# Query norms in a one-core transformer block: the squares move through TensorE instead of being its weights

## The chip, the cores and the metric

The kernel runs on one core of one Trainium2 chip. The metric is the device time of one execution in microseconds (us); the time before is the median of three runs, 1139.22 us (1139.1 to 1141.05). A profile is taken of one execution. Its engines are TensorE (PE; its weight loads are listed as PEld), VectorE (DVE), ScalarE (ACT), GpSimd (POOL) and SyncE (SP), which here only issues DMAs. A matrix product on TensorE has a stationary operand, which is loaded first, and a moving one, which streams through it column by column; results go to one of eight banks of PSUM, from which VectorE and ScalarE read. [...]

## The reference

A block of 512 tokens and 1024 features: a gated feed-forward layer, a mixer, another feed-forward layer. In the mixer two attentions ("moba" and "dsa", eight heads of 64 each) work on projections of the normed input. The change concerns how the queries of both are normed:

```python
qa = rmsnorm(qa.reshape(B, S, N_HEADS_DSA, HEAD_DIM), q_norm_dsa[l])
qb = rmsnorm(qb.reshape(B, S, N_HEADS_MOBA, HEAD_DIM), q_norm_moba[l])
# rmsnorm(x, g) = x * rsqrt(mean(x * x, over the 64 of a head) + EPS) * g
```

Everything is float32. In "dsa" each query attends to its best keys by a second score (128 of them), in "moba" to blocks of keys; both add a bias by distance and take a softmax.

## The kernel before, in words

Activations lie with features on partitions and the 512 tokens along the free dimension. A product in float32 precision is made of three products in the faster fp32r type: operands are split into a rounded high part and the remaining low part (`mm3`, lines 125 to 128: high x high, high x low, low x high). Weights come by DMA into `raw` (three buffers, `wunit`, line 121), ScalarE rounds them into `whi` (line 111), and GpSimd subtracts to get `wlo` (line 117), in the attentions in pieces of 256 columns. A projection `unit` (line 389) is eight such triplets into one PSUM bank, and `post` then reads the bank out.

PSUM's eight banks form rings: `mm` has three (projections and the key norms' sums), `s` two (the logits of the attention), `pt` two (transposes, the query norms' sums, small things), `o` one. A scratch ring of SBUF, `tmp`, has seven buffers of 128x512 (TMPS, line 30); a tile is given back when its last reader is done. Who wants a tile while none is free waits.

TensorE's instructions stand in the order in which the program is written (line 85). `weave` (line 712) interleaves the attention's logits, transposes and values with the steps of a list of projections, the filler. One step is one triplet of a projection (two in the value units), and each step ticks a clock (`tick`, line 379). `later(n, fn)` runs `fn`, and so puts its TensorE instructions there, n steps after now. The instructions of the other engines and SP are put in an order by a planner with modelled times and priorities ahead of the run, and each engine then executes its own strictly in that order: an instruction that waits holds all behind it.

Each head pair of each attention has one key unit and one query unit, eight query units in all. `k_post` (line 462) squares the keys, splits the squares into two parts, and after LAG = 11 steps two products of 512 columns with the block matrix `bd` (1/64 on each head's diagonal block, lines 475 and 476) give the means, spread over all partitions. `q_post` (line 426) is different: the norm isn't applied to q. q goes unnormed into the logits, and the factor of each query enters in the softmax step (`f`, a scale in line 628) and its inverse in the bias addend (`inv`, lines 602 to 605). Both are needed with queries on partitions. So LAG_Q = 4 steps after `q_post`, `norm` (line 438) uses each 128x128 block of the squares as the stationary operand and two columns of `bd` as the moving one, in plain float32; sums of queries on partitions, for both heads of the pair, then stand in a `pt` bank, 128x8. Six small VectorE instructions (lines 444 to 451) and two ScalarE ones turn them into `f` and `inv`.

The softmax sums at line 628 feed the exponential, the transposes (line 659, `turn`) and the values (lines 680 and 681). Row sums of the softmax take a way through DRAM already: `norms` (line 633) writes a row (line 642) and reads it back spread over partitions (line 646).

Of the kernel before, what the change touches and what calls it, by code (L numbers as in the profile page):

```python
# [11 lines left out]
F32 = mybir.dt.float32  # L12
F32R = mybir.dt.float32r
AF = mybir.ActivationFunctionType
ALU = mybir.AluOpType

P = 128
S = 512
D = 1024
F = 2816  # L20
DH = 64
# [4 lines left out]
NQ = S // P  # L26
# [5 lines left out]

PIN, EVERY = (0, 20, 28, 31), 2

LAG, LAG_Q = 11, 4

SPIN, HURRY = 10, 200

# [7 lines left out]
def f32(ap):  # L46
    return ap.bitcast(F32)
# [3 lines left out]
def block_kernel(ctx, tc, x, gains, wgu1, wd1, w_in, w_v, wb_a, wb_b, w_out, wgu2, wd2, rel_bias, onehot, out):  # L51
    nc = tc.nc

    def pool(name, bufs=1, **kw):
        return ctx.enter_context(tc.tile_pool(name=name, bufs=bufs, **kw))
# [4 lines left out]
    dr = pool("dr", space=bass.MemoryType.DRAM)  # L60
# [21 lines left out]
    def log_exp(out, src, fn, **k):  # L82
        table_op("natural_log_exp_and_others", out, src, fn, **k)
# [3 lines left out]
    def T(tag, bufs, shape=(P, S), dt=F32, p=sb):  # L87
        uid[0] += 1
        return p.tile(list(shape), dt, tag=tag, name=f"{tag}{uid[0]}", bufs=bufs)

    def tmp(dt=F32):
        return T("tmp", TMPS, (P, S), dt)

    def mmps():
        return T("mm", 3, p=ps)
# [4 lines left out]
    def tps():  # L100
        return T("pt", 2, p=ps)
# [60 lines left out]
    bd = cp.tile([P, P], F32R, name="bd")  # L162
# [27 lines left out]
    def blocks(a):  # L190
        return a.rearrange("p (t c) -> p t c", c=P)

    def rev(a):

        o = a[:, P - 1:P]
        return bass.AP(o.tensor, o.offset, [list(o.ap[0]), [P, NQ], [-1, P]])
# [49 lines left out]
    whole, halves = (slice(0, S),), (slice(0, S // 2), slice(S // 2, S))  # L246
# [129 lines left out]
    def later(n, fn):  # L376
        late.append((steps[0] + n, fn))
# [48 lines left out]
    def q_post(p, gain, dst):  # L426


        sq = tmp()
        nc.scalar.activation(blocks(sq), rev(p), AF.Square)  # L430
        q = T("q", 2, (P, 2, S), F32R)
        for e, h1 in enumerate(HALF):
            h2, g = HALF[1 - e], gain[h1]
            nc.scalar.activation(blocks(q[h1, e, :]), rev(p)[h1], AF.Copy, scale=g)
            nc.vector.scalar_tensor_tensor(blocks(q[h2, e, :]), rev(p)[h1], g, blocks(f32(q)[h1, e, :]),
                                           op0=ALU.mult, op1=ALU.subtract)

        def norm():
            pv = tps()[:, 0:2 * NQ]
            for t in range(NQ):  # L440
                nc.tensor.matmul(pv[:, 2 * t:2 * t + 2], sq[:, t * P:(t + 1) * P], f32(bd)[:, 0:P:DH],
                                 start=True, stop=True)
            w, y, b, f, inv = (a for a in T("fq", 3, (P, 5, 2 * NQ)).rearrange("p n c -> n p c"))
            nc.vector.tensor_mul(w, pv, r2q[:, 1])
            log_exp(y, w, AF.Ln, bias=epst)
            log_exp(y, y, AF.Exp, scale=-0.5)
            nc.vector.scalar_tensor_tensor(b, w, EPS, y, op0=ALU.add, op1=ALU.mult)
            nc.vector.tensor_mul(b, b, y)
            nc.vector.scalar_tensor_tensor(b, b, -3.0, y, op0=ALU.add, op1=ALU.mult)
            nc.vector.scalar_tensor_tensor(f, b, -0.5, r2q[:, 0], op0=ALU.mult, op1=ALU.mult)  # L450
            nc.vector.reciprocal(inv, f)
            dst.extend([q, f, inv])

        later(LAG_Q, norm)

    lows = [cp.tile([P, 2, S], F32R, name=f"low{i}") for i in range(2)]
    for low in lows:
        for e in range(2):
            nc.gpsimd.memset(f32(low)[HALF[1 - e], e, :], 0.0)
    turns = [0, 0]  # L460

    def k_post(p, gain, dst):

# [61 lines left out]
    def qk_units(br, pr, q, k):  # L525
        u = (U_QA, U_QB)[br] + pr
        g = 2 * br
        return [proj(u + 4, lambda p: k_post(p, gqk[:, g + 1:g + 2], k)),
                proj(u, lambda p: q_post(p, gqk[:, g:g + 1], q))]
# [237 lines left out]
    p = tps()  # L767
# [9 lines left out]
    for e in range(2):  # L777
        nc.vector.tensor_copy(r2q[:, 0, e:2 * NQ:2], p[:, NQ:2 * NQ])
    nc.vector.tensor_mul(r2q[:, 1], r2q[:, 0], r2q[:, 0])
    q_post(ps3[0], gqk[:, 2:3], moba[0][0])  # L780
    k_post(ps3[1], gqk[:, 3:4], moba[0][1])
    run(v0)
# [35 lines left out]
    for c in range(KD):  # L818
        g1 = opened(c)
        ma = tmp()  # L820
        w = ready.pop(0)
# [88 lines left out]
```

## Time and profile before

| | |
|---|---|
| median of three runs | 1139.22 us (1139.1 to 1141.05) |
| profiled execution | 1139.47 us, span 1137.7 us |
| PE busy | 1130.0 us, 5364 products |
| PEld busy | 947.0 us |
| DVE, ACT, POOL busy | 646.2, 469.9, 549.3 us |
| DMA | 111.73 MB, mean 98 GB/s |
| eight query norms | between 385 and 664 us |

The span is the time from the first to the last instruction of the profiled execution. Matrix products are pipelined, and the ends that the profile shows are modelled; what a product costs TensorE is read from the distance of its start to the start of the next one. A row of the time-ordered view has the start, the length, the engine, the line, the tiles it writes and reads, the shape and a count; a bracket at its end has the engine's idle time before it and the instruction that ended it.

### The profile page before, as it was taken

What the parts mean: (1) busy time and instruction counts of PE and PEld (TensorE: products, weight loads), DVE (VectorE), ACT (ScalarE), POOL (GpSimd) and SP (SyncE); (2) the same over time, 40 slices, a digit from 0 to 9 for tenths busy, and PEclk for the clock granted to TensorE, in tenths of its full rate; (3) what the DMA queues carried; (4) which work ended last, traced back from release to release, by engine and by line L of the source; (5) the groups of instructions that cost most, each with busy time, mean ns of one, the idle gap of its engine ahead of it and who ended that gap; (6) DMA issues with size and microseconds to landing.
All of it is one profiled execution on the core that took longest, in us unless ns stands there. A gap on an engine that the chain in (4) does not pass through costs nothing.

```text
span 1137.7 us, 14242 instructions
## 1 busy us (share of the span) xinstructions
PE 1130.0 (99%) x5364; PEld 947.0 (83%) x5364; DVE 646.2 (57%) x971; ACT 469.9 (41%) x770; POOL 549.3 (48%) x435
## 2 busy tenths in 40 slices
PE   9999999999999999999999999999999999999998
PEld 8888888888888888888889888888888888888887
DVE  6853156613557458699958785754663156613641
ACT  6432123312325568768238766444332123212321
POOL 3444444444446574665564551174444444444443
PEclk9999999999999999999999999999999999999999
DMA  7233222322323222321232321422233232322322
GB/s 237 94 118 95 93 97 105 95 93 93 106 71 114 83 101 84 102 75 52 98 131 93 110 67 47 139 93 97 103 98 93 93 105 100 93 93 96 104 70 102
DMA packets 39580, 111.73 MB, mean 98 GB/s; under 512 B 4534, under 2 KB 9048, under 8 KB 39512
## 3 DMA queue, kind: packets, MB, share of 16 engines
q1 hardware_dynamic: 39080, 110.28, 29.4%
q8 instruction: 42, 0.69, 0.2%
q10 hardware_dynamic: 432, 0.55, 0.2%
q14 instruction: 26, 0.21, 0.1%
HBM read 108.64 MB, written 2.17 MB: 97 GB/s over the span
## 4 chain that ended last, share of the span: by engine, by line
PE 92%; DVE 5%; ACT 2%; issue 1%; POOL 1%; POOLq 0%; DVEq 0%
PE mm L126 22%; PE mm L127 22%; PE mm L128 22%; PE s L126 7%; PE s L128 7%; PE s L127 7%; PE pt L659 1%; DVE l L628 1%; PE s L619 1%; PE s L620 1%; DVE work L566 1%; PE o L681 1%; PE o L680 1%; POOL wlo L117 1%; DVE pt L670 0%
## 5 line engine op out<-in xcount | busy, mean ns | idle before, releaser
L117 POOL TENSOR_TENSOR wlo<-raw,whi 128x256 fp32r<-128x256 f32 (+2 forms) x344 | 491.6, 1449 | 528.7 <-ACT whi L111 517.4
L111 ACT ACTIVATE whi<-raw 128x1024 fp32r<-128x1024 f32 (+2 forms) x206 | 203.8, 994 | 509.5 <-PE mm L127 325.8
L126 PE MATMUL mm<-x,whi 128*128 128x512 f32 x630 | 249.6, 396 | 1.1 <-DVE v L501 1.1
L128 PE MATMUL mm<-x,wlo 128*128 128x512 f32 x630 | 245.9, 390 | 0.0
L127 PE MATMUL mm<-x,whi 128*128 128x512 f32 x630 | 245.9, 390 | 0.0
L126 PE MATMUL mm<-a,whi 128*128 128x512 f32 (+1 forms) x462 | 178.5, 386 | 0.0
L127 PE MATMUL mm<-a,whi 128*128 128x512 f32 (+1 forms) x462 | 178.5, 386 | 0.0
L128 PE MATMUL mm<-a,wlo 128*128 128x512 f32 (+1 forms) x462 | 178.4, 386 | 0.0
L128 PEld LDWEIGHTS mm<-x,wlo 128*128 128x128 f32 x630 | 118.2, 188 | 25.3
L126 PEld LDWEIGHTS mm<-x,whi 128*128 128x128 f32 x630 | 118.4, 188 | 22.8 <-DVE v L501 1.6
L127 PEld LDWEIGHTS mm<-x,whi 128*128 128x128 f32 x630 | 118.5, 188 | 21.3 <-DVE x L207 0.4
L126 PE MATMUL s<-x,whi 128*128 128x512 f32 x342 | 133.1, 389 | 0.0
L128 PE MATMUL s<-x,wlo 128*128 128x512 f32 x342 | 133.0, 389 | 0.0
L127 PE MATMUL s<-x,whi 128*128 128x512 f32 x342 | 133.0, 389 | 0.0
L289 DVE SCALAR_TENSOR_TENSOR h<-mm,h 128x512 f32<-128x512 f32 (+1 forms) x49 | 33.3, 681 | 167.6 <-PE mm L128 167.6
L275 DVE TENSOR_TENSOR tmp<-tmp,tmp 128x512 f32<-128x512 f32 x44 | 97.0, 2205 | 30.4 <-ACT tmp L75 30.1
L154 DVE TENSOR_TENSOR a<-tmp,a 128x512 fp32r<-128x512 f32 x49 | 86.4, 1764 | 28.5 <-ACT a L153 28.3
L126 PEld LDWEIGHTS mm<-a,whi 128*128 128x128 f32 x462 | 86.8, 188 | 17.6
L127 PEld LDWEIGHTS mm<-a,whi 128*128 128x128 f32 x462 | 86.8, 188 | 17.6
L128 PEld LDWEIGHTS mm<-a,wlo 128*128 128x128 f32 x462 | 86.8, 188 | 17.6
L128 PEld LDWEIGHTS s<-x,wlo 128*128 128x128 f32 x342 | 64.2, 188 | 13.4
L126 PEld LDWEIGHTS s<-x,whi 128*128 128x128 f32 x342 | 64.2, 188 | 13.3
(196 smaller groups left out, 1361.8 us busy)
## 6 DMA issues: line engine op xcount, KB each, us to landing
raw<-in_ffn_w_gu_dram SPq DMA_DIRECT2D x84, 512.0 KB, 3.5
raw<-in_w_in_dram SPq DMA_DIRECT2D x35, 512.0 KB, 3.5
raw<-in_ffn_w_down_dram SPq DMA_DIRECT2D x32, 512.0 KB, 3.5
raw<-in_ffn_w_down_dram SPq DMA_DIRECT2D x16, 384.0 KB, 3.1
bias<-fd SPq DMA_DIRECT2D x16, 256.0 KB, 3.4
raw<-in_w_v_dram SPq DMA_DIRECT2D x8, 512.0 KB, 3.4
raw<-in_w_out_dram SPq DMA_DIRECT2D x8, 512.0 KB, 3.5
raw<-in_ffn_w_gu_dram SPq DMA_DIRECT2D x16, 128.0 KB, 3.9
```

The costliest lines, as they stand in the source:

```text
L111: nc.scalar.activation(hi, raw, AF.Copy)
L117: eng.tensor_sub(lo[:, b], raw[:, b], f32(hi)[:, b])
L126: nc.tensor.matmul(pt, wh, xh, start=start, stop=False)
L127: nc.tensor.matmul(pt, wh, xl, start=False, stop=False)
L128: nc.tensor.matmul(pt, wl, xh, start=False, stop=stop)
L154: nc.vector.tensor_sub(lo, src, f32(hi))
L275: nc.vector.tensor_mul(g1, g1, s)
L289: nc.vector.scalar_tensor_tensor(h[c][:, b], pd, 0.5, h[c][:, b], op0=ALU.mult, op1=ALU.add)
L566: nc.vector.match_replace(out=acc, in_to_replace=m8, in_values=acc, imm_value=-2e38)
L619: nc.tensor.matmul(p[:, 0:N], qb, k[:, e, 0:N], start=True, stop=False)
L620: nc.tensor.matmul(p[:, 0:N], qb, kl[:, e, 0:N], start=False, stop=True)
L628: sums[i] = nc.vector.tensor_tensor_reduce(out=pe, in0=p[:, 0:W], in1=pe, scale=f[:, 2 * qt + e:2 * qt + e + 1], scalar=3e38, op0=ALU.add, ...
```

## The change

The squares are now split in a high and a low part, as for the keys: ScalarE copies them to fp32r, GpSimd subtracts in two halves. After seven steps instead of four, the two parts move, 512 columns each, against the two columns of `bd`; the result is 2x512, a head per partition, in a bank of the `mm` ring. ScalarE copies it to SBUF, SP writes it to one of two DRAM rows, and four steps later `factors` reads it back by two DMAs, one element a piece, to 128x8 in SBUF. The rest of the arithmetic is unchanged.

```diff
-LAG, LAG_Q = 11, 4
+LAG, LAG_Q, LAG_R = 11, 7, 4
...
         sq = tmp()
         nc.scalar.activation(blocks(sq), rev(p), AF.Square)
+        sh, sl = tmp(F32R), tmp(F32R)
+        nc.scalar.activation(sh, sq, AF.Copy)
+        for b in halves:
+            nc.gpsimd.tensor_sub(sl[:, b], sq[:, b], f32(sh)[:, b])
...
         def norm():
-            pv = tps()[:, 0:2 * NQ]
-            for t in range(NQ):
-                nc.tensor.matmul(pv[:, 2 * t:2 * t + 2], sq[:, t * P:(t + 1) * P], f32(bd)[:, 0:P:DH],
-                                 start=True, stop=True)
-            w, y, b, f, inv = (a for a in T("fq", 3, (P, 5, 2 * NQ)).rearrange("p n c -> n p c"))
+            p2 = mmps()[0:2, :]
+            for a in (sh, sl):
+                nc.tensor.matmul(p2, bd[:, 0:P:DH], a, start=a is sh, stop=a is sl)
+            sums2 = tmp()[0:2, :]
+            nc.scalar.activation(sums2, p2, AF.Copy)
+            row = qrows_d[turns[2] % 2]
+            turns[2] += 1
+            nc.sync.dma_start(row, sums2)
+            later(LAG_R, lambda: factors(row))
+
+        def factors(row):
+
+            pv, w, y, b, f, inv = (a for a in T("fq", 3, (P, 6, 2 * NQ)).rearrange("p n c -> n p c"))
+            a = row[0:1, :]
+            for e in range(2):
+                nc.sync.dma_start(pv[:, e:2 * NQ:2], bass.AP(a.tensor, a.offset + e * S, [[1, P], [P, NQ]]))
             nc.vector.tensor_mul(w, pv, r2q[:, 1])
...
-    turns = [0, 0]
+    turns = [0, 0, 0]
+    qrows_d = [dr.tile([2, S], F32, name=f"qrow{i}") for i in range(2)]
```

## Rows read from the trace of the kernel before

**Rows 1.** The page, busy time by engine (share of the span) and instructions

```profile
PE 1130.0 (99%) x5364; PEld 947.0 (83%) x5364; DVE 646.2 (57%) x971; ACT 469.9 (41%) x770; POOL 549.3 (48%) x435
```

**Rows 2.** Waits of PE, 380 to 720 us: total us, times, longest

```profile
PE mm L126 <- DVE v L501: 1.1, 1, 1.1
PE s L619 <- DVE st L628: 0.7, 1, 0.7
PE pt L659 <- DVE pt L670: 0.6, 1, 0.6
PE pt L441 <- ACT tmp L430: 0.5, 1, 0.5
```

**Rows 3.** Busy times by stretch; behind POOL: PEclk, DMA share, GB/s

```profile
380.00:530.00 150.00, 147.62 (x863) 128.68 (x862) 113.89 (x284) 107.65 (x231) 95.40 (x126) 1.00 0.27 88
```

**Rows 4.** PE in order of time around the second query norm

```profile
424.22 0.39 PE L475 MATMUL mm<-tmp,bd 128*128 128x512 f32 x1
...
424.68 0.49 PE L659 MATMUL pt<-ident,l 128*128 128x128 f32 x3
...
425.71 0.95 PE L441 MATMUL pt<-bd,tmp 128*128 128x2 f32 x8
426.52 0.47 PE L126 MATMUL mm<-x,whi 128*128 128x512 f32 x1
426.83 0.39 PE L127 MATMUL mm<-x,whi 128*128 128x512 f32 x1
...
427.53 0.39 PE L126 MATMUL mm<-x,whi 128*128 128x512 f32 x1
```

**Rows 5.** ACT in order of time, the fifth norm's squares

```profile
522.86 0.60 ACT L430 ACTIVATE tmp<-mm 128x512 f32<-128x512 f32 x1 [0.75 <-DVE os L687]
```

**Rows 6.** Groups by shape (busy us, mean ns); then ACT and POOL near 423 us

```profile
L469 ACT ACTIVATE tmp<-tmp 128x512 fp32r<-128x512 f32 x8 | 5.0, 620 | 0.4 <-DVE tmp L466 0.4
L117 POOL TENSOR_TENSOR wlo<-raw,whi 128x256 fp32r<-128x256 f32 x212 | 169.2, 829 | 139.3 <-ACT whi L111 133.3 <-PE s L620 4.3 <-issue 1.7
...
423.11 0.58 ACT L430 ACTIVATE tmp<-mm 128x512 f32<-128x512 f32 x1
...
422.69 2.83 POOL L117 TENSOR_TENSOR wlo<-raw,whi 128x256 fp32r<-128x256 f32 x4 [1.50 <-ACT whi L111]
```

**Rows 7.** POOL and DVE in order of time near 483 us

```profile
483.32 1.30 POOL L690 TENSOR_TENSOR os<-os,rb 128x512 f32<-128x512 f32 x1 [3.98 <-DVE os L687]
...
483.54 1.62 DVE L478 SCALAR_TENSOR_TENSOR tmp<-tmp,tmp 128x512 f32<-128x512 f32 x1
```

**Rows 8.** Waits of DVE, 380 to 720 us

```profile
DVE l L628 <- PE s L620: 18.5, 13, 5.0
```

**Rows 9.** SP's issues in order of time; an issue group (KB, us to landing); SP's waits

```profile
444.42 0.33 SPq L642 DMA_DIRECT2D row<-rw  x1
447.33 1.14 SPq L646 DMA_DIRECT2D rb<-row  x2
...
gT<-in_gains_dram ACTq DMA_DIRECT2D x1, 22.0 KB, 2.3
...
SPq L121 <- POOL wlo L117: 772.8, 184, 9.7
```

**Rows 10.** DVE in order of time, from the second norm to the third

```profile
426.69 0.17 DVE L444 TENSOR_TENSOR fq<-pt,r2q 128x8 f32<-128x8 f32 x1 [0.94 <-PE pt L441]
426.89 0.76 DVE L435 SCALAR_TENSOR_TENSOR q<-mm,gqk,q 64x512 fp32r<-64x512 f32 x1
...
437.29 0.20 DVE L451 RECIPROCAL fq<-fq 128x8 f32<-128x8 f32 x1
...
442.21 0.33 DVE L628 CUSTOM_DVE_ANT_0 l<-s,l,fq 128x128 f32<-128x128 f32 x1
...
445.31 0.17 DVE L444 TENSOR_TENSOR fq<-pt,r2q 128x8 f32<-128x8 f32 x1
...
450.99 0.20 DVE L451 RECIPROCAL fq<-fq 128x8 f32<-128x8 f32 x1
```

## The prediction

> **What bounds the kernel now.** I read the page's busy shares first, then TensorE's waits, then the stretch in which five of the eight query norms fall, then the engines around single norms. TensorE is busy for 99% of the span [rows 1]. From 380 to 720 us it waits for another engine only a few times, 2.9 us in the four rows shown [rows 2]. [...] So what TensorE no longer has to issue comes off the end nearly one for one, and what is added elsewhere costs only where it makes TensorE wait.
>
> **What TensorE loses and gains.** The old product has the squares as its stationary operand, in plain fp32: a norm shows as 8 products of 2 columns, each behind a weight load of its own. A group starts at 425.71 and the next product at 426.52, so it takes 0.81 us; the product behind it takes 0.31 us (to 426.83), where a 512-column one next to it has 0.23 (below) [rows 4]. I count 0.89 us a norm; all eight groups look like this one. 8 x 0.89 = 7.1 us go.
>
> In their place come two products of 512 columns with a 2-column stationary operand. The trace has no such shape. The nearest is the key norm's pair: 512 columns too, against all 128 columns of the same block matrix. It starts at 424.22 and the transposes after it at 424.68: 0.46 us for both [rows 4]. Lower end: the pace of the old 2-column products, 0.81 / 8 = 0.10 each, 0.2 for both. Upper end: the 0.89 of the old group, if a load of an odd shape breaks the pace as that did. I take 0.46, because what streams is the same. 8 x 0.46 = 3.7 us come. Net: -3.4 us (bounds -5.5 and 0).
>
> **Stalls that may go.** At the fifth norm TensorE stands 0.5 us, because the squares are late (the wait of line 441), and 0.6 us at the transposes after it, for a bank of their ring (line 659) [rows 2]. The squares were late because ScalarE waited 0.75 us for the reader of a scratch tile [rows 5]: the seven `tmp` buffers were all in use. After the change the product comes three steps later and takes no bank of the transposes' ring, but it needs two more scratch tiles and two GpSimd subtractions first. What is late next is the low half of the squares. I take half of the 1.1 us: -0.6 us (bounds -1.1, and +1.1 if they double).
>
> **Work added beside TensorE.** Each norm gains on ScalarE a copy of 128x512 (0.62 us, the key norm's rounding square) and one of 2x512 (at most the same) [rows 6]: 8 x 1.24 = 9.9 us, on an engine that is 72% busy [rows 3]. GpSimd gains 16 subtractions of 128x256 at 0.83 us [rows 6], 13.3 us, at 64% busy. VectorE keeps its six small instructions. The idle quarter of the two engines hides this, as long as nobody waits behind it in order. For the low half: squares from 423.11 to 423.69, copy to 424.3, GpSimd busy with a weight's four pieces until 425.5 [rows 6], two subtractions to 427.2. The product, three steps after 425.71, is due no earlier than 428.5, since one step takes about 1.0 us (426.52 to 427.53) [rows 4]. So 1.3 us are spare and I cost it at nothing; with one more weight of 2.8 us ahead of it on GpSimd it would cost 1.5 us a norm.
>
> GpSimd's longer hours have a second price. A VectorE instruction with two inputs in SBUF began at 483.54, 0.22 us after a GpSimd one of 1.30 us, and took 1.62 us: it ended 0.5 us after that one [rows 7]. [...]
>
> **The factors come later.** Today the sums lie in PSUM when the group ends. New are a copy (0.6 us), the row's write, and its read by two DMAs. A row's write now is issued at 444.42 and the read of it, which waits for the landing, at 447.33: 2.9 us, and that is the upper end for one small DMA; the lower end is the 2.3 us of the gains' load [rows 9]. The second read is issued half a microsecond behind the first (1.14 for two [rows 9]). So 0.6 + 2.3 to 2.9 + 0.5 + 2.3 to 2.9 is 5.7 to 6.9 us; reads of 512 pieces of 4 bytes have no row, so I take 6.5 and leave the upper end open to one DMA more, 9. While SP waits for the landing, weight loads wait behind it, up to 2.9 us. They wait anyway, mostly for GpSimd to free a buffer, 773 us in 184 waits [rows 9], so I cost this at nothing; without that cover each norm could cost 2.9 us.
>
> A norm's first VectorE instruction thus comes 3 (steps) + 6.5 = 9.5 us later. Behind it in VectorE's queue stand softmax sums and bank readouts, and TensorE behind those. Who needs the factors? The first attention's second pair multiplies at 426.69, has its reciprocals at 437.49, and its first softmax sum runs at 442.21 [rows 10]. The third pair needs 5.9 us for the same chain (445.31 to 451.19), against 10.8 here, where other work stood between. With 9.5 us more at the start, the second pair's chain ends at 426.7 + 9.5 + 5.9 = 442.1, about when its sum is due; with the stretched chain it is 4.8 us late, with a still shorter one not at all. The fourth pair repeats this pattern with a little more room; the others are used far later. For both together: 0 to 9 us, and I take 1.0, since the other work that stretched the chain (the key norm's) is done by then.
>
> **The bank.** The product's bank now is one of the main ring's three. At the product, one bank holds the running unit, one the key norm's sums, and the third was the query's own projection, whose last reading ends at 426.89 + 0.76 = 427.65 [rows 10]; a copy more on ScalarE makes it 428.3. The product is due at 428.5, so it just fits. I take 0.2 us in two norms, 0.4 us; upper end: in each of eight norms the one wait at a unit's head that there is now, 1.1 us [rows 2], 8.8 us.
>
> **Sum.** The profiled execution took 1139.47 us (span 1137.7 and 1.8 around it), 0.25 over the median of 1139.22. 1139.47 - 3.4 - 0.6 + 1.0 + 0.4 = 1136.9; the 0.25 off again, 1136.6 us, 2.6 below the median.
>
> **Rivals.** (a) The gain is eaten by small waits of the order of those that stand there now (0.5 to 1.1 us each [rows 2]): three or four more, 3 us, give 1139.6. For it: the scratch ring was already full once [rows 5], and each norm now holds two tiles for seven steps and a third through the row's write. Against: TensorE felt that only once.
>
> (b) Slower: VectorE stands in its queue for the row. Its order is fixed ahead; if the multiply is placed where the row is thought to land, and it lands later, the softmax sums behind it are held, and TensorE with them, since the logits have two banks. It decides when the delay passes what VectorE has spare, 18.5 / 13 = 1.4 us [rows 8]. With a return of 9 us instead of 6.5 it passes by 1.1 us, in the six norms inside an attention 6.6 us: 1136.6 + 6.6 = 1143.2. Against: today's reads of the rows by GpSimd show no such wait. [...]
>
> (c) The 2-column operand does not stream: 0.89 us for both products makes TensorE's gain nil, 1136.6 + 3.4 = 1140.0.
>
> **Numbers.** Forecast 0.54, its own range 1134.0 (both stalls gone, no new wait, and a little under 0.46 us a pair) to 1138; (a) 0.24, (b) 0.15, (c) 0.07. 0.2% is 2.3 us, about what a measurement of this kernel tells from no change. Faster than 1136.9 holds most of the forecast, 0.50; slower than 1141.5 most of (b) and a tail of (a), 0.18; the same 0.32. The range reaches from 1134.0 to 1141.8, short of (b)'s middle.
>
> **What would show it.** Right: 16 products of 2x512, 0.23 us apart, for the 64; no TensorE wait for the low half; reciprocals of pairs two and four just ahead of their softmax sums; shorter waits near 523. Wrong: VectorE idle in front of the multiply by a DMA, TensorE waiting for softmax sums around pairs two and four, TensorE waiting at a norm or a unit's head for a main-ring bank, or ScalarE waiting for scratch tiles.

## The result and the profile after

The changed kernel takes 1149.9 us (median of four, 1149.06 to 1151.06) against 1139.95 us beside it: a ratio of 1.0089, 95% interval 1.0076 to 1.0102. It is slower by about 10 us, where 3 us faster was forecast; the range ended at 1141.8. The profiled execution took 1149.38 us, span 1147.3 us, 9.6 us more than before.

The first row answers to [rows 1], the second to [rows 3].

```profile
PE 1129.3 (98%) x5316; PEld 941.9 (82%) x5316; DVE 647.4 (56%) x971; ACT 478.0 (42%) x786; POOL 555.8 (48%) x451
```

```profile
380.00:530.00 150.00, 145.00 (x817) 123.35 (x815) 109.82 (x274) 107.70 (x231) 101.76 (x136) 1.00 0.28 87
```

TensorE has 48 products less and is hardly less busy in sum, and in the stretch of the five norms it now stands 5.0 us of 150, not 2.4. The two new products do stream as was taken, one pair from 606.74 to 607.20, 0.46 us (TensorE in order of time):

```profile
606.51 0.39 PE L128 MATMUL mm<-x,wlo 128*128 128x512 f32 x1
606.74 0.63 PE L445 MATMUL mm<-tmp,bd 128*2 128x512 f32 x2
607.20 0.49 PE L675 MATMUL pt<-ident,l 128*128 128x128 f32 x3
```

So the gain of 3.4 us is there, and some 13 us of newly lost time stand against it. I worked this out over the whole trace: for each pair of neighbouring products the distance of their starts less that trace's median distance after a product of as many columns, summed. That is 10.8 us before and 23.8 us after: 13.0 more, and 13.0 - 3.4 = 9.6, the difference of the spans. Below I call this sum TensorE's lost time. The low half of the squares, the wait that the prediction looked out for, held TensorE once, 0.3 us at 447. TensorE's waits (total us, times, longest; 380 to 720 us as in [rows 2]) name most of the rest:

```profile
PE pt L675 <- DVE pt L686: 4.3, 2, 2.3
PE s L635 <- DVE st L644: 1.8, 3, 0.9
PE mm L126 <- DVE v L517: 1.8, 1, 1.8
PE mm L445 <- DVE q L439: 1.7, 1, 1.7
PE s L635 <- ACT tmp L563: 1.1, 1, 1.1
PE mm L126 <- ACT tmp L447: 0.9, 1, 0.9
PE pt L654 <- DVE recip L653: 0.5, 2, 0.3
```

Three places carry it, and each is an in-order queue with something new in it.

**ScalarE, 612 and 668 us.** The transposes of line 675 wait twice for their bank. ScalarE in order of time, first after, then before:

```profile
607.76 0.57 ACT L447 ACTIVATE tmp<-mm 2x512 f32<-2x512 f32 x1
608.23 0.25 ACT L685 ACTIVATE pt<-pt 128x128 fp32r<-128x128 f32 x1
608.39 1.05 ACT L111 ACTIVATE whi<-raw 128x1024 fp32r<-128x1024 f32 x1
...
610.64 2.20 ACT L501 ACTIVATE k<-tmp,gqk 64x512 fp32r<-64x512 f32 x3
612.75 0.36 ACT L685 ACTIVATE pt<-pt 128x256 fp32r<-128x256 f32 x1
```

```profile
604.21 0.28 ACT L669 ACTIVATE pt<-pt 128x128 fp32r<-128x128 f32 x1
604.38 1.05 ACT L111 ACTIVATE whi<-raw 128x1024 fp32r<-128x1024 f32 x1
605.34 0.37 ACT L669 ACTIVATE pt<-pt 128x256 fp32r<-128x256 f32 x1
...
606.64 2.94 ACT L485 ACTIVATE k<-tmp,gqk 64x512 fp32r<-64x512 f32 x4
```

The copy of the second transposed block (128x256) stood ahead of the four key copies; now, with the 0.57 us copy of the sums (line 447) in the order, it stands behind them, and so it does at 668. VectorE reads the same bank after it, and TensorE stands:

```profile
614.09 0.42 DVE L686 TENSOR_TENSOR pt<-pt,pt 128x256 fp32r<-128x256 f32 x1
```

```profile
614.65 0.63 PE L675 MATMUL pt<-ident,l 128*128 128x128 f32 x4 [1.98 <-DVE pt L686]
```

The two places lose 2.14 and 2.45 us, and behind the first the granted clock falls for some products, 1.6 us more (last section): 6.2 us.

**The main ring's bank, fifth norm.** The product waits for VectorE's last reading of the query's own projection, and then the next unit for the copy of the sums:

```profile
530.95 0.63 PE L445 MATMUL mm<-tmp,bd 128*2 128x512 f32 x2 [1.69 <-DVE q L439]
...
533.14 0.39 PE L126 MATMUL mm<-whi,x 128*128 128x256 f32 x1 [0.86 <-ACT tmp L447]
```

Lost there: 1.85 + 1.02 = 2.9 us.

**SyncE, second norm.** The row is written at 429.84, and its read is issued at 434.95: not for the landing, but because a bias table's load stands between them and waits for GpSimd. VectorE then stands 2.50 us in front of the multiply, with a softmax sum behind it, and ScalarE 3.33 us in front of the factors' logarithm, with a reader of a logit bank (line 563) behind it, for which TensorE waits 1.1 us (SyncE's issues, then its wait for GpSimd; VectorE; ScalarE):

```profile
429.84 0.25 SPq L450 DMA_DIRECT2D qrow<-tmp  x1
434.58 0.33 SPq L365 DMA_DIRECT2D bias<-fd  x1
434.95 0.98 SPq L458 DMA_DIRECT2D fq<-qrow  x2
...
SPq L365 <- POOL l L621: 4.4, 1, 4.4
```

```profile
439.76 0.17 DVE L459 TENSOR_TENSOR fq<-fq,r2q 128x8 f32<-128x8 f32 x1 [2.50 <-DMA fq<-qrow]
439.90 0.75 DVE L644 CUSTOM_DVE_ANT_0 l<-s,l,fq 128x512 f32<-128x512 f32 x1
...
441.74 0.20 DVE L466 RECIPROCAL fq<-fq 128x8 f32<-128x8 f32 x1
```

```profile
439.96 0.30 ACT L75 ACTIVATE fq<-fq,epst 128x8 f32<-128x8 f32 x1 [3.33 <-DVE fq L459]
440.17 0.36 ACT L563 ACTIVATE tmp<-s 128x256 f32<-128x256 f32 x1
```

From 439 to 466 TensorE loses 3.5 us in four waits for logit banks and softmax sums (1.22, 0.35, 0.85, 1.12), against one of 0.9 us before. Only the first stands right behind the row. The others may be an echo of it, since VectorE next waits for copies of the ScalarE that stood for the row (0.83 us at 442.93), or lateness of other work; no run separates these.

### The profile page after: what moved, and what is told of

It reads as the page before. It is cut to its first block, busy times and chain, and to the rows that moved or that the text cites. A ratio compares the mean times of both kernels' runs of the same rounds, so it can differ in the third digit from the quotient of the medians.

```text
span 1147.3 us, 14227 instructions
## 1 busy us (share of the span) xinstructions
PE 1129.3 (98%) x5316; PEld 941.9 (82%) x5316; DVE 647.4 (56%) x971; ACT 478.0 (42%) x786; POOL 555.8 (48%) x451
## 4 chain that ended last, share of the span: by engine, by line
PE 88%; DVE 5%; ACT 4%; POOL 1%; issue 1%; DMA 1%; SPq 0%; DVEq 0%; ACTq 0%; POOLq 0%
PE mm L126 21%; PE mm L127 21%; PE mm L128 21%; PE s L126 7%; PE s L128 7%; PE s L127 7%; DVE l L644 1%; PE pt L675 1%; ACT l L75 1%; ACT tmp L75 1%; ACT k L501 1%; POOL wlo L117 1%; DVE work L582 1%; ACT whi L111 1%; PE o L697 1%
## 5 line engine op out<-in xcount | busy, mean ns | idle before, releaser
L117 POOL TENSOR_TENSOR wlo<-raw,whi 128x256 fp32r<-128x256 f32 (+2 forms) x344 | 486.4, 1433 | 537.0 <-ACT whi L111 525.0
L128 PEld LDWEIGHTS s<-x,wlo 128*128 128x128 f32 x342 | 64.2, 188 | 13.4
```

What stands on the lines that cost most here:

```text
L117: eng.tensor_sub(lo[:, b], raw[:, b], f32(hi)[:, b])
L128: nc.tensor.matmul(pt, wl, xh, start=False, stop=stop)
```

## The experiments

Every ratio is to the kernel before, run on the same chip beside it. Five theories stand against each other: the route through DRAM, the bank and the step of the product, ScalarE's order, the added load, and SyncE's order.

**1. The route through DRAM.** *e1_no_dram*: four transposes on TensorE take the sums to queries on partitions.

```diff
-            nc.sync.dma_start(row, sums2)
...
+            pv = tps()[:, 0:2 * NQ]
+            for t in range(NQ):
+                nc.tensor.transpose(pv[:, 2 * t:2 * t + 2], sums2[:, t * P:(t + 1) * P], ident[0:2, 0:2])
...
```

> The changed kernel without the way through DRAM: the sums, copied to SBUF as before, get to queries on partitions by four small TensorE transposes per norm into a bank of the transposes' ring, four steps after the products; the split squares, the two 512-column products and their main-ring bank stay. Theory A (VectorE and ScalarE stand in their queues for the row to come back, and TensorE behind them): the waits after norms 2, 6, 7 and 8 go, TensorE pays 32 transposes at 0.07 to 0.11 us, some 3 us; time 1140 to 1143 us. Theory B (the main-ring bank): the 1.8 and 1.0 us at norm 5 stay and the rest too, 1148 or more. Theory C (the added copies and subtractions, which shift the order of all engines): 1146 or more.

Measured: 1154.09 us, 1.0125 [1.0108, 1.0142]. The fifth norm's wait stays; near 612 and 670 the new transposes stand in the same queue for the same late readers, longer than before:

```profile
PE pt L454 <- DVE pt L682: 6.7, 2, 3.5
PE mm L445 <- DVE q L439: 1.7, 1, 1.7
```

*e2_dram_alone*: the kernel before, with its eight small products and four steps, but the sums sent through DRAM.

```diff
+            sums8 = T("s8", 2, (P, 2 * NQ))
+            nc.scalar.activation(sums8, pv, AF.Copy)
+            nc.sync.dma_start(row, sums8)
...
```

> The kernel before with the way through DRAM alone: old products with the squares as weights, four steps after the projection, in the transposes' ring; their 128x8 sums are copied to SBUF, written to DRAM, read back by two DMAs of 512 pieces of 4 bytes, factors four steps later. Theory A: slower by most of what the change lost plus what the products had won, 1148 to 1152 us, with VectorE idle by the DMA in front of the multiply. Theory B: no main-ring bank is taken, so 1139 to 1142. Theory C: no added split, so 1139 to 1143.

Measured: 1142.2 us, 1.0019 [1.0009, 1.0029]; VectorE waits once for the row, 1.0 us. The route alone costs about 2 us, not 10.

**2. The bank and the steps.** *e3_pt_bank*: the product's bank from the transposes' ring (`tps()` for `mmps()`).

> The changed kernel with the products' bank taken from the transposes' ring of two, as before, and not from the main ring. Theory B: the waits of 1.8 and 1.0 us near 530 and the shorter one near 449 go, 3.2 us of 1149.9, so 1146 to 1147, if the transposes don't wait for that bank in their turn. Theory A: 1148 to 1151, the waits after norms 2, 6 and 8 stay.

Measured: 1151.59 us, 1.0098 [1.0083, 1.0113]. The fifth norm's loss shrinks to 0.7 us, but at the second norm there are new waits for the transposes' ring: the product waits 1.5 us for it, the values (line 697) 1.9. *e5_lag7*: the kernel before with only its small products three steps later (`LAG_Q = 7`).

> The kernel before with its query norm's products seven steps after the projection in place of four, nothing else. Theory A and B: the factors come only some 3 us later and nobody waits, 1138 to 1141 us. Theory C in the form that the place of the products in the order alone moves the time: 1143 or more.

Measured: 1149.0 us, 1.0078 [1.0063, 1.0093]. The shift alone costs 9 us in the kernel before. The small products now want a bank of the transposes' ring while VectorE still has to read a transposed block there, and 3.0 us of the 9 are time at the lower clock:

```profile
PE pt L441 <- DVE pt L670: 6.4, 4, 2.7
```

*e6_lag4*: the changed kernel at four steps (`LAG_Q = 4`).

> The changed kernel with its products four steps after the projection, as before, in place of seven; route through DRAM, split and main-ring bank as changed. Theory D (the three steps later are the cost: the factor chain of the queries no longer runs among the key norm's chain, which shifts the order of VectorE and ScalarE, and the products meet other holders of their bank): 1140 to 1144 us, the waits of 2.1 and 2.4 us at transposes near 612 and 668 gone. Theory A' (the DRAM route and the later products together): 1147 or more. A cost of its own: the low half may not be ready at four steps, up to 1 us a norm.

Measured: 1154.77 us, 1.013 [1.0115, 1.0145]. At four steps the main ring's bank isn't free in seven of eight norms:

```profile
PE mm L445 <- DVE q L439: 12.9, 7, 4.2
```

*e9_no_dram_lag4*: four steps, and the transposes of e1.

> Split squares and two 512-column products four steps after the projection, the sums by four TensorE transposes per norm instead of DRAM. Theory D: 1138 to 1141 us (products 3.2 us less, transposes some 3 us more, waits as before). If the late products were not the cost but the split's copies and subtractions: 1146 or more.

Measured: 1165.17 us, 1.0217 [1.0202, 1.0233]; 13.1 us of the same wait, and 4.7 us at line 671. In the main ring an early product meets a bank that is still being read; in the transposes' ring the later one of e5 does.

**3. ScalarE's order.** *e7_turn_first*: the two copies of transposed blocks go ahead by priority. *e8_before_turn_first*: the same in the kernel before.

```diff
-                nc.scalar.activation(dst(pth), src, AF.Copy)
-                nc.vector.tensor_sub(dst(ptl), src, dst(f32(pth)))
+                with tc.high_priority(HURRY):
+                    nc.scalar.activation(dst(pth), src, AF.Copy)
+                    nc.vector.tensor_sub(dst(ptl), src, dst(f32(pth)))
```

> The changed kernel with one line around the two copies of each transposed softmax block that gives them the same planner's priority as the softmax sums have. Theory D in the form that the planner puts four 0.73 us key copies ahead of them on ScalarE: the two waits of 2.1 and 2.4 us and the 1.6 us of half clock behind the first go, 1143 to 1145 us. If the waits come from VectorE standing for the row: no change, 1149 to 1151.

> The kernel before with the same line, as the control of the run with this line in the changed kernel: theory D 1139 to 1141 us (there the copies stand ahead of the key copies anyway). If it gains 3 us or more here too, that line is worth something by itself and its gain in the changed kernel tells nothing of the change.

Measured: 1146.85 us, 1.0057 [1.004, 1.0073], and 1141.47 us, 1.0015 [1.0005, 1.0024]. In e7 both waits are gone and some 3 us with them, not the 6 that hung on them. TensorE's longest waits of e7 from 600 to 680 us are now

```profile
PE mm L126 <- DVE v L517: 2.3, 1, 2.3
PE mm L126 <- DVE tmp L229: 0.4, 1, 0.4
```

and behind the first of these, and behind the waits of the fifth norm, the granted clock falls, where in the changed kernel it stays at 1.00 (rows as in [rows 3]):

```profile
532.00:535.50 3.50, 3.04 (x13) 3.04 (x14) 3.47 (x10) 1.92 (x5) 0.00 (x0) 0.52 0.25 56
645.00:648.00 3.00, 3.00 (x7) 2.42 (x8) 3.00 (x8) 2.49 (x5) 0.78 (x1) 0.50 0.01 1
```

That costs 3.1 us, against 1.6 in the changed kernel; the rest of the lost time falls by 3.8 us (table below).

*e10_copy_dve*: the sums' copy on VectorE.

```diff
-            nc.scalar.activation(sums2, p2, AF.Copy)
+            nc.vector.tensor_copy(sums2, p2)
```

> The changed kernel with one word changed: the 2x512 copy of the sums (line 447) runs on VectorE instead of ScalarE. In ScalarE's planned order both copies of transposed blocks now stand ahead of the four key copies in the groups near 612 and 668 us. If the copy's place in ScalarE's order is what makes the two transposes there wait, both waits (2.1 and 2.4 us) go, the granted clock stays high at 615 to 619, and the time falls from 1149.9 to 1144 to 1146, as with the copies ahead by priority (1146.9) or a little better. If what counts is ScalarE's and VectorE's sheer load, the copy is only shifted to VectorE and the time stays at 1148 to 1151. The main-ring bank's wait at 528 to 533 (2.9 us) is not touched by either.

Measured: 1149.41 us, 1.0085 [1.007, 1.01]. Half the expectation held: the waits at 612 and 668 are gone, so the copy's place in ScalarE's order made them. The time did not follow, and 2.7 us of what is lost is now the lower clock. The second norm's copy now stands in VectorE's queue until 431.70, 3 us behind its product; the row is written at 434.38, behind a bias load that waits 8.4 us for GpSimd, and read at 436.46, behind a weight's load, and the chain of the third place ends in one wait of 4.0 us near 443 (VectorE in order of time, then TensorE's wait):

```profile
440.85 0.43 DVE L459 TENSOR_TENSOR fq<-fq,r2q 128x8 f32<-128x8 f32 x1 [2.25 <-DMA fq<-qrow]
```

```profile
PE s L635 <- DVE st L644: 4.0, 1, 4.0
```

*e11_lag8*: eight steps (`LAG_Q = 8`); in its trace the copies of the blocks stand ahead of the key copies again. *e13_copy_dve_lag8*: both.

> The changed kernel with the product at eight steps behind the projection instead of seven; nothing else. In ScalarE's planned order both copies of transposed blocks again stand ahead of the key copies at 612 and 668. If the bank's wait at the fifth norm is a matter of the product coming just too early for the reader of the query's own projection (four steps: 14 us of waits, seven: 2.9 us), eight steps take most of the 2.9 away; together with the two waits at 612 and 668 gone, 1142 to 1145. If the scratch tiles that are held a step longer are what hurts, new waits for scratch and for late reciprocals appear and the time is 1149 or more.

> Both together: the sums' copy on VectorE and the product at eight steps. Meant to beat the changed kernel and, if the two causes (ScalarE's order at 612 and 668, the bank at the fifth norm) are all there is besides small waits, the kernel before as well: 1149.9 less 6 for the first and 2 to 2.9 for the second is 1141 to 1142; with small waits of the second pair's late factors gone too, 1139. If the waits are only moved by each shift of the order, as with transposes in place of the path through DRAM, it stays at 1145 or more.

Measured: 1145.9 us, 1.0048 [1.0032, 1.0065], and 1151.44 us, 1.0102 [1.0087, 1.0117]. In e11 the waits at 612 and 668 are gone and the product's own wait at the fifth norm falls to 0.6 us, but the waits for softmax sums rise to 4.1 us in four. The two edits don't add: in e13 the long wait of e10 is back, 4.3 us, and 4.4 us go to the lower clock, against 1.5 in e11.

**4. The added load.** *e12_no_low* asks where the cost lies, in the split or in the order: no low half, so no rounding copy, no subtractions and two scratch tiles less (the high half is counted twice in its place).

```diff
...
-        sh, sl = tmp(F32R), tmp(F32R)
-        nc.scalar.activation(sh, sq, AF.Copy)
-        for b in halves:
-            nc.gpsimd.tensor_sub(sl[:, b], sq[:, b], f32(sh)[:, b])
+        sh = sl = tmp(F32R)
+        nc.scalar.activation(blocks(sh), rev(p), AF.Square)
...
```

> The changed kernel without the low half of the squares (the output loses that accuracy): the squares are rounded once, both products take the same tile, and the rounding copy on ScalarE, the two GpSimd subtractions and two of the three scratch tiles of each norm go. In ScalarE's order the sums' copy still stands ahead of the key copies and the second copy of transposed blocks behind them near 668, not near 612. [...] If it lies in where the product, its bank and its copy stand in order, it falls only by the waits that hang on the low half (0.3 to 0.8 us near 447 and 480) and the one at 612, some 3 to 4 us: 1145 to 1147.

Measured: 1149.64 us, 1.0083 [1.0068, 1.0098], not told apart from the changed kernel. 5 us of ScalarE (8 x 0.62) and 12 us of GpSimd (16 x 0.76) less gain nothing; the waits are still there, the one for the bank longer:

```profile
PE pt L671 <- DVE pt L682: 4.3, 2, 2.2
PE mm L441 <- DVE q L435: 2.6, 1, 2.6
```

The expected 3 to 4 us did not come either: both waits of the transposes are still there.

**5. SyncE's order.** *e14_read_first*: the read is put right behind the write, and each later load of a weight or a bias table behind the read. *e15*: the same with eight steps; *e16*: with e7's edit; *e17*: all three.

```diff
+    def behind_read(load):
+        if back[0] is not None:
+            tc.add_manual_dep(load.ins, back[0].ins.name, NOSYNC, reason="row first")
...
-        nc.sync.dma_start(raw, src)
+        behind_read(nc.sync.dma_start(raw, src))
...
```

> The changed kernel with one edit: in SyncE's queue the read of the sums' row stands right behind its write; every load of a weight or a bias table that comes later in the program is held behind it. If SyncE's order is what makes VectorE stand for the row, the row is back some 6 to 8 us after the product in every norm instead of 10.5 to 11.5 in the second, VectorE's waits for it (4.6 us, the longest 2.5) fall under 1.5 us in all, the score's wait at 439 goes, and the time falls by 2 to 4 us to 1146 to 1148; the two waits for the transposed blocks at 612 and 668 may stay. If the row's latency is the DMA's own (landing of pieces of 4 bytes), VectorE's waits stay and the time is 1149 to 1151. If loads that are held behind the row starve TensorE, it waits for weights (L126 by GpSimd or a DMA) and the time goes above 1152.

> The same edit on the changed kernel with the product at eight steps (1145.9 without it, VectorE's waits for the row 4.8 us). If SyncE's order is a cause by itself, the time falls by 2 to 4 us to 1142 to 1144, and TensorE's 4.8 us of waits for the softmax sums halve. If each shift only moves the waits, it stays at 1145 or more.

> The same edit together with the copies of transposed blocks ahead by priority, product at seven steps (1146.85 without the edit, VectorE's waits for the row 5.0 us). If the three causes add (ScalarE's order at 612 and 668, SyncE's order, the bank at the fifth norm) this has only the last and small ones: 1143 to 1145. If the waits are only moved: 1146 or more.

> All three: read right behind the write, copies of transposed blocks ahead by priority, product at eight steps. Meant to beat both kernels: with no more waits than the kernel before had, 3.3 us under it, 1136 to 1138; with 3 to 5 us of small waits left, 1139 to 1142. If a wait for the main ring's bank at the fifth norm (2 to 3 us) and late factors of the second pair remain whatever the order, 1143 or more.

Measured: 1201.28 us, 1.0543 [1.0526, 1.056]; 1224.07, 1.0733 [1.0717, 1.0749]; 1202.15, 1.0546 [1.053, 1.0562]; 1215.23, 1.0653 [1.0635, 1.0671]. The part about the row came out: in e14 the second norm's read follows its write by 1.2 us, and VectorE waits for the row 0.9 us in all. The third theory, that held loads starve TensorE, decided the time (SyncE's issues; waits of SyncE, TensorE and VectorE):

```profile
437.94 0.25 SPq L456 DMA_DIRECT2D qrow<-tmp  x1
439.16 0.93 SPq L460 DMA_DIRECT2D fq<-qrow  x2
```

```profile
SPq L456 <- ACT tmp L453: 74.9, 6, 27.5
...
PE mm L132 <- ACT whi L111: 46.9, 8, 10.7
...
DVE fq L465 <- DMA fq<-qrow: 0.9, 1, 0.9
```

The edit held back loads that had stood ahead of the write too; the write itself then waited up to 27.5 us at the head of SyncE's queue for its sums, with the weights behind it. Its price is this edit's, not the change's. *e18_read_by_act* therefore issues the two reads from ScalarE's queue, at seven steps, and *e19_read_by_act_lag8* at eight.

```diff
-                nc.sync.dma_start(pv[:, e:2 * NQ:2], bass.AP(a.tensor, a.offset + e * S, [[1, P], [P, NQ]]))
+                nc.scalar.dma_start(pv[:, e:2 * NQ:2], bass.AP(a.tensor, a.offset + e * S, [[1, P], [P, NQ]]))
```

> The changed kernel with the two reads of the row issued from ScalarE's queue instead of SyncE's; nothing else. The weights' loads keep their order. If the row stood behind loads in SyncE's queue, the second norm's row is read some 4 us sooner, VectorE's waits for it (4.6 us) fall to 2 or less and the time falls by 1 to 3 us, to 1147 to 1149; the transposed blocks' waits near 612 and 668 stay, since their copies' place in ScalarE's order stays. If ScalarE now stands for the write's landing (1 us each) or pays for the issues (up to 1 us a norm), its copies come later and TensorE's waits grow: 1151 or more.

> The same with the product at eight steps, where the transposed blocks' copies stand ahead of the key copies. The best guess for a version that beats both: 1145.9 less the 2 to 4 us that TensorE waits for softmax sums behind the row, 1142 to 1144. If the waits are only moved again: 1145 or more; level with the kernel before (1139 to 1141) only if the bank at the fifth norm goes as well.

Measured: 1150.78 us, 1.0097 [1.008, 1.0114], and 1145.01 us, 1.0041 [1.0026, 1.0056]. In e18 VectorE's waits for the row fall to 2.5 us, but the second norm's read is issued at 434.90, no sooner than before: ScalarE has its own queue of work ahead of it. The softmax sums hold TensorE 4.4 us, more than the 1.8 of the changed kernel. e19 is level with e11 and the best of the variants with the two products. None beats the kernel before. The remaining waits of e19 are these:

```profile
PE s L635 <- DVE st L644: 3.6, 4, 2.2
PE mm L126 <- DVE v L517: 2.5, 2, 2.2
PE s L635 <- ACT tmp L563: 2.0, 1, 2.0
...
PE mm L126 <- ACT tmp L447: 1.0, 1, 1.0
```

**The account.** TensorE's lost time, worked out as above; the part of it at the lower clock (products at a granted clock of 0.50 that wait for nobody, their distance over the median); the rest, which is mostly waits; and the ratio:

| kernel | lost us | clock | rest | ratio |
|---|---|---|---|---|
| before | 10.8 | 0 | 10.8 | 1 |
| route alone (e2) | 13.4 | 0 | 13.4 | 1.0019 |
| small products at seven steps (e5) | 19.9 | 3.0 | 16.9 | 1.0078 |
| changed | 23.8 | 1.6 | 22.2 | 1.0089 |
| no DRAM (e1) | 29.1 | 6.8 | 22.3 | 1.0125 |
| blocks' copies first (e7) | 21.5 | 3.1 | 18.4 | 1.0057 |
| copy on VectorE (e10) | 23.8 | 2.7 | 21.1 | 1.0085 |
| eight steps (e11) | 21.1 | 1.5 | 19.6 | 1.0048 |
| copy on VectorE, eight steps (e13) | 24.8 | 4.4 | 20.4 | 1.0102 |
| no low half (e12) | 25.0 | 2.9 | 22.1 | 1.0083 |
| reads by ScalarE, eight steps (e19) | 18.7 | 0 | 18.7 | 1.0041 |
| four steps (e6) | 28.9 | 2.8 | 26.1 | 1.013 |

More scratch tiles, or a bank and tiles for the norm alone, were not tried. The rings take eight banks of PSUM (3 + 2 + 2 + 1); whether SBUF has room for more tiles, no run shows.

## Why the prediction was wrong

- **TensorE's gain, -3.4 us: right.** 0.46 us a pair, streaming as the key norm's does; rival (c) falls.
- **Load beside TensorE, 0 us: right as to load, wrong in its condition.** ScalarE's 9.6 us (8 x 0.62 and 8 x 0.58) and GpSimd's 12 us are hidden: e12 takes most of that away and gains nothing. VectorE is busy 647.4 us against 646.2, 1.2 us more beside GpSimd's 12: the instruction of [rows 7] took 1.62 us there and 0.68 to 0.69 at six of its line's seven other places (1.05 at one), and in the changed kernel it takes 0.67 to 0.69 at all eight. What failed is the step "hides this, as long as nobody waits behind it in order": I priced the idle quarter of ScalarE and never looked at who stands behind the new copy. At 612 and 668 it was a transposed block with its bank, 6.2 us with the clock. That this place is the cause is shown by e7 and e10, which take the waits away by different means.
- **The bank, +0.4 us: mis-sized, 2.9 us.** I took both the due time and the reading from the second norm. At the fifth norm a step is shorter (two triplets of 256 columns in a value unit, 6 x 0.12 = 0.7 us against about 1.0), but other products stand between, and the product isn't due sooner: 8.3 us behind the start of the projection's last product (520.81 to about 529.1), against 7.2 at the second norm (421.17 to 428.32). What is late is the reading. ScalarE, held by a scratch tile's reader among others, begins the squares 5.7 us behind that product, at the second norm 1.9 (423.07), and from the squares to VectorE's last reading it takes 4.4 us (526.52 to 530.89), as at the second norm (4.5 in [rows 6, 10]). [rows 5] had shown these late squares; I used them for the stalls and not for the bank. e6 shows what the seven steps avoid (12.9 us of waits); the 9 us of e5 belong to the transposes' ring, which the changed product doesn't use (TensorE, then ScalarE, changed kernel):

```profile
520.81 0.40 PE L128 MATMUL mm<-x,wlo 128*128 128x512 f32 x1
...
526.52 0.60 ACT L430 ACTIVATE tmp<-mm 128x512 f32<-128x512 f32 x1 [0.75 <-DVE os L703]
```

- **The factors, +1.0 us: the end was right by luck, the mechanism not.** The second pair's reciprocals come at 441.74, done at 441.94, forecast 442.1. But the multiply began 3.6 us later than forecast (439.76, not 426.7 + 9.5 = 436.2), and the chain behind it took 2.2 us, not 5.9; the two errors cancel. I had the row's own DMA as the long part and only asked what waits behind it in SyncE's queue. With the read right behind the write, write and read take 4.0 us (e14's first norm, written at 391.56, multiplied at 395.56, with VectorE waiting for it), less than the 5.1 to 6.3 I had for them. In the changed kernel's second norm they took 9.9 us (429.84 to 439.76), and 4.8 us of that (430.09 to 434.91) went to the bias load ahead of the read, which waited 4.4 us for GpSimd. Another 4.8 us was the read, from its issue to the multiply that stood for it (434.95 to 439.76), against 2.8 in e14 (392.78 to 395.56), where other loads were held back; what makes it longer in the changed kernel no run separates. And I followed VectorE alone: ScalarE's two instructions of the factors wait in order as well, 3.33 us.
- **Rival (b): its mechanism is there** (VectorE stands 4.6 us for the row, the softmax sums behind it), but what stands right behind it costs TensorE 1.2 us at the second norm, where I had 1.1 in each of six. It isn't the main part: e2 has the route for 2 us, and without it e1 loses as much as the changed kernel, clock left out (22.3 and 22.2 us in the table). The reads of 512 pieces of 4 bytes each are inside those 4.0 us in e14; whether the size of the pieces has a part in the longer reads of the changed kernel, no run tells.
- **Rival (a), small waits that eat the gain, comes nearest**, but I had three or four of 0.5 to 1.1 us in it; six of the new losses are 1.0 to 2.5 us each.
- **Stalls that may go, -0.6 us: they went, by 1.1** (0.36 us of lost time is left near 523 of 1.5). But the wait for the main ring's bank came at the same norm, and it is longer.
- **The sum's form was wrong.** I added local terms. The runs show that they don't add: e7 takes away 6.2 us and gains 3; e10 takes the same away and gains nothing; e13 joins two edits, is slower than e11 and no faster than e10. Part of this is the clock: without it e7 gains 3.8 us, but the lower clock took back 1.5, and in e13 it takes 4.4. The rest is order: that of ScalarE, VectorE, GpSimd and SyncE is planned as a whole, and each new instruction shifts waits elsewhere.

**What stays open.** The three places explain 6.2, 2.9 - 1.1 (the part of the old waits near 523 that went) and 3.5 - 0.9 = 2.6 us of the 13.0; 1.0 us lies at line 322 near the start, which the change doesn't touch, and the rest in small waits. Why no variant gets under 18.7 us of lost time isn't settled. That the kernel before simply has a good order, which any edit upsets, fits e5 and e8, which change the order alone and cost 9 and 1.7 us, but two edits don't show it for any. Nor is it settled what decides whether the clock falls behind a wait.

## What to carry to other kernels

In a kernel that keeps TensorE 99% busy and gives every other engine a fixed order, "the engine has room" is no price: go to each place where a new instruction will stand, and ask which bank, tile or load of the engine that bounds the kernel is behind it, in SyncE's queue as on the engines. For a DMA that returns to the same kernel, look first at what stands between its write and its read. A gain of a few tenths of a microsecond per place on the bounding engine is smaller than one such displaced wait, here 2 us; forecast its sign with that in mind.

## What the runs showed of the hardware

After the wait of 1.98 us at 612 the granted clock fell to about half (0.58 as a mean from 615 to 619 us, 0.50 from 616 to 619): products of 512 columns started 0.43 us apart instead of 0.23, 1.6 us in all. In the same stretch of the kernel before it is 1.00. After a wait of 2.29 us, at 668, it stayed at 1.00; after one of 2.3 us in e7 it fell; after the 4.0 us wait of e10 it was 0.50 from 446 to 450. The length of the wait alone doesn't tell. The first is the row of after (time, then the busy engines as in [rows 3], PEclk behind POOL), the second of e10:

```profile
615.00:619.00 4.00, 4.00 (x14) 3.33 (x13) 3.20 (x8) 1.30 (x5) 0.91 (x1) 0.58 0.55 138
```

```profile
446.00:450.00 4.00, 3.32 (x15) 3.35 (x16) 3.17 (x8) 3.04 (x9) 1.83 (x5) 0.50 0.19 68
```

A wait can thus cost nearly twice what it shows (2.14 and 1.6 us), and two kernels are only compared rightly with this part taken apart: it is 0 to 6.8 us in the table above. And loading only two columns of weights didn't break the pace of the stream: 0.23 us from one product to the next, as with 128.
